# A decoder block's head: parameters packed into the first load, squared tiles summed as they come, root and broadcast ahead of the adaLN rows

## The chip, the core and the metric

The kernel runs on one NeuronCore of a Trainium2 chip. Its engines work side by side, each through its own list of instructions in order: TensorE (PE in the rows: matmuls, with the loads of their stationary operand listed as PEld), VectorE (DVE), ScalarE (ACT), GpSimd (POOL), and SyncE (SP), which here issues nearly all transfers. Sixteen DMA engines move data between HBM and on-chip memory (SBUF); matmuls write to PSUM. An engine waits at an instruction until what the instruction needs is there, and all that stands behind it on that engine waits too. The metric is the device time of one execution in microseconds, lower is better.

## What is computed

One block with an attention-and-convolution mixer and a gated convolutional FFN; 256 positions of 1024 features, all float32. Each half normalises its input and modulates it by a conditioning vector c:

```python
mod = silu(c) @ w_ada[l] + b_ada[l]
sh1, sc1, gt1, sh2, sc2, gt2 = jnp.split(mod[:, None, :], 6, axis=-1)
h = rmsnorm(x, g_mix[l]) * (1.0 + sc1) + sh1          # x / sqrt(mean(x*x) + eps) * g
proj = h @ w_in[l]                                    # q, k, v, u, c_gate, b_gate
...                                                   # attention, short convolution, two norms
x = x + gt1 * (mixed @ w_out[l])
h = rmsnorm(x, g_ffn[l]) * (1.0 + sc2) + sh2
up = causal_dwconv(h @ w_up[l], ffn_conv_w[l], ffn_conv_b[l])
x = x + gt2 * ((silu(gte) * val) @ w_down[l])
return rmsnorm(x, g_final)
```

## The kernel before

Everything lies feature-major: x is `xT`, 128 partitions by 8 tiles of 256 positions. Weights come as 1 MB pieces (q/k/v pieces 768 KB) into a ring of 8 slots; `advance()` issues the next piece on SyncE as soon as the slot it goes to is freed, in the order of the list `order`. At the start that is: adaLN weights of group 0 (`a1`), `wqkv` of tile 0 (q0), `a1` of group 1, q1, two pieces of `a1` for group 2, q2, q3. The first eight pieces are issued at once, q0 and q1 in two transfers each (columns 0 to 1023, then 1024 to 1535). Ahead of them go x in four quarters of two tiles (L91), and, on ScalarE's queue, the first 104 columns of the parameter array `pp` (L90: c, biases, norm weights); its other 176 columns, for the FFN, are loaded at L388.

Large matmuls keep float32 accuracy by splitting each operand into a rounded part (hi) and a rest (lo), and doing three passes: hi*hi, hi*lo, lo*hi (`mm3`). hi is a cast on ScalarE (`split_hi`, `split_hi_q`, or `hhi` for the activations), lo a subtraction on VectorE (`split_lo`, `split_lo_q`, `hlo`). A plain float32 matmul leaves two records in the trace.

The head works as follows. Each engine's order is the order of the statements, since the program is scheduled by hand.
- `keep_clock(n)` runs n matmuls of a constant on TensorE whose result nobody reads; 22 of them at the start.
- ScalarE makes silu(c) (`cs`, L232); VectorE repeats it over 32 columns (`crep`) and adds 1 to two bias columns (`bsc1`). ScalarE squares x a quarter at a time (L242), VectorE adds the quarters up to one tile (L244, L245).
- `ada_rows(g)` (L253): 64 matmul records for shift and scale of one group of tiles; groups are (0), (1), (2, 3), (4, 5), (6, 7). `ada_cols(g)` (L266) turns the rows into columns on VectorE: one transpose and three small operations.
- `add_squares` (L210) sums over the partitions on TensorE; `rms_root` (L216) does the scaling on VectorE and the power -0.5 on GpSimd; `rms_bcast` (L223) spreads the result with two matmuls into PSUM (`psrx`).
- `normed(kt)` multiplies a tile by it on VectorE, `modulated(kt)` makes `hhi` on ScalarE and `hlo` on VectorE.

The order of the statements at L338 to L352 is: rows of group 0, sum of squares, root, columns of group 0, `keep_clock(4)`, three casts and one subtraction for q0, broadcast, `normed(0)`, `modulated(0)`, a copy of the broadcast to SBUF (`rxb`), two more subtractions. Then the loop over the 8 tiles starts (L354): q/k matmuls, with the rows of a later group between them, v matmuls, and the splits of the next tile. `normed(1)` to `normed(7)` read `rxb`.

Of the kernel before, what the change touches and what calls it, by code (L numbers as in the profile page):

```python
# [8 lines left out]
F32 = mybir.dt.float32  # L9
F32R = mybir.dt.float32r  # L10
AF = mybir.ActivationFunctionType
OP = mybir.AluOpType
AX = mybir.AxisListType.X

P = 128
S = 256
D = 1024
A = 512
# [4 lines left out]
KT = D // P  # L23
# [4 lines left out]
PC = {}  # L28
_n = 0
for _name, _w in (("c", 8), ("b_ada", 48), ("g_mix", 8), ("g_ffn", 8), ("g_mixed", 8), ("g_fin", 8),  # L30
                  ("conv_w", 12), ("conv_b", 4), ("ffn_w", 3 * 2 * NJ), ("ffn_b", 2 * NJ)):
    PC[_name] = _n
    _n += _w
NP = _n


FFN_SEQ = [("v", 0), ("g", 0), ("v", 1), ("g", 1), ("v", 2), ("g", 2)]
# [20 lines left out]
def decoder_block(ctx: ExitStack, tc, xT_in, pp, ada1, ada2, wqkv, wst, out):  # L58
# [5 lines left out]
    nc = tc.nc  # L64
    ACT, DVE, PE, POOL = nc.scalar, nc.vector, nc.tensor, nc.gpsimd

    cp = ctx.enter_context(tc.tile_pool(name="cp", bufs=1))
# [15 lines left out]
    def p1(tag, name):  # L83
        return ps1.tile([P, 512], F32, tag=tag, name=name)


    xT = cp.tile([P, KT, S], F32, name="xT")
    par = cp.tile([P, NP], F32, name="par")
    ffn_par = slice(PC["ffn_w"], NP)
    nc.scalar.dma_start(par[:, 0:PC["ffn_w"]], pp[:, 0:PC["ffn_w"]])  # L90
    for i in range(4):  # L91
        nc.sync.dma_start(xT[:, 2 * i:2 * i + 2, :], xT_in[:, 2 * i:2 * i + 2, :])

    def col(name, i):
        o = PC[name] + i
        return par[:, o:o + 1]


    order = []
# [10 lines left out]
    def advance():  # L110
        while state["next"] < len(order):
            i = state["next"]
            if i >= NRAW and order[i - NRAW] not in freed:
                return
            k = order[i]
            t = rawp.tile([P, 2048], F32, tag="raw", name="raw")
            if k[0] == "a1":
                nc.sync.dma_start(t, ada1[GROUPS[k[1]][k[2]]])
            elif k[0] == "q":
                for c in ((slice(0, 2 * A), slice(2 * A, 3 * A)) if k[1] <= 1 else (slice(0, 3 * A),)):  # L120
                    nc.sync.dma_start(t[:, c], wqkv[k[1], :, c])
            elif k[0] == "a2":
                nc.sync.dma_start(t, ada2[k[1], k[2]])
            else:
                nc.sync.dma_start(t, wst[k[1]])
            ring[k] = t
            state["next"] += 1

    def free(k):
        freed.add(k)  # L130
        advance()

    advance()


# [17 lines left out]
    def keep_clock(n, ps=warm):  # L153
        for _ in range(n):
            PE.matmul(ps[:, 0:P], ones, ones, start=True, stop=True)

    keep_clock(22)


    def split_hi(raw, n=1024):  # L160
# [49 lines left out]
    def add_squares(ss, s2, first, last):  # L210

        for t in range(2):
            PE.matmul(ss[:, t * REP:(t + 1) * REP], s2[:, t * P:(t + 1) * P], ones[:, 0:REP], start=(first and t == 0), stop=last,  # L213
                      skip_group_check=True)
# [20 lines left out]
    bsc1 = cp.tile([P, 2, KT], F32, name="bsc1")  # L235
    DVE.tensor_scalar(bsc1[:, 0, :], par[:, PC["b_ada"] + 8:PC["b_ada"] + 16], 1.0, None, op0=OP.add)
    DVE.tensor_scalar(bsc1[:, 1, :], par[:, PC["b_ada"] + 32:PC["b_ada"] + 40], 1.0, None, op0=OP.add)

    pss = p1("v", "pss")
    sqx = cp.tile([P, KT, S], F32, tag="mix", name="sqx")  # L240
    for i in range(4):
        ACT.activation(sqx[:, 2 * i:2 * i + 2, :], xT[:, 2 * i:2 * i + 2, :], AF.Square)  # L242
        if i:
            DVE.tensor_add(sqx[:, 0:2, :], sqx[:, 0:2, :], sqx[:, 2 * i:2 * i + 2, :])  # L244
    DVE.tensor_add(sqx[:, 0, :], sqx[:, 0, :], sqx[:, 1, :])  # L245
    rxb = cp.tile([P, S], F32, tag="sqs0", name="rxb")

    hT = (cp.tile([P, KT, S], F32R, name="hhi"), cp.tile([P, KT, S], F32R, name="hlo"))
    mod1 = cp.tile([P, 2, KT], F32, name="mod1")
# [3 lines left out]
    def ada_rows(g):  # L253


        n = len(GROUPS[g])
        AR[g] = pw(f"psr{g}")[:, 0:64 * n]
        for k in range(KT):
            a = ring["a1", g, k * n // KT].rearrange("p (k j c) -> p k j c", j=4, c=64 * n)
            for j in range(4):  # L260
                PE.matmul(AR[g][32 * j:32 * j + 32, :], crep[:, k, :], a[:, k % (KT // n), j, :],  # L261
                          start=(k == 0), stop=(k == KT - 1))
            if (k + 1) % (KT // n) == 0:
                free(("a1", g, k * n // KT))

    def ada_cols(g):  # L266

        n, kts = len(GROUPS[g]), slice(GROUPS[g][0], GROUPS[g][-1] + 1)
        tr = wk.tile([P, 256], F32, tag="tr", name=f"tr{g}")[:, 0:64 * n]
        DVE.transpose(tr, AR[g])  # L270
        v = tr.rearrange("p (n s q) -> p n s q", s=2, q=32)[:, :, :, 0]
        b = PC["b_ada"] + kts.start
        DVE.tensor_tensor(mod1[:, 0, kts], v[:, :, 1], bsc1[:, 0, kts], op=OP.add)
        DVE.tensor_mul(mod1[:, 0, kts], mod1[:, 0, kts], par[:, PC["g_mix"] + kts.start:PC["g_mix"] + kts.stop])
        DVE.tensor_tensor(mod1[:, 1, kts], v[:, :, 0], par[:, b:b + n], op=OP.add)

    XN = {}
# [11 lines left out]
    def normed(kt, rb):  # L289
        XN[kt] = wk.tile([P, S], F32, tag="xn", name=f"xna{kt}")  # L290
        DVE.tensor_mul(XN[kt], xT[:, kt, :], rb)

    def modulated(kt):
        sc, sh = mod1[:, 0, kt:kt + 1], mod1[:, 1, kt:kt + 1]
        ACT.activation(hT[0][:, kt, :], XN[kt], AF.Identity, bias=sh, scale=sc)
        hf = wk.tile([P, S], F32, tag="cu", name=f"hf{kt}")
        DVE.tensor_scalar(hf, XN[kt], sc, sh, op0=OP.mult, op1=OP.add)
        DVE.tensor_sub(hT[1][:, kt, :], hf, hT[0][:, kt, :].bitcast(F32))
# [6 lines left out]
    def new_q(kt):  # L305
        WQ[kt] = [hip.tile([P, 1024], F32R, tag=t, name=t) for t in ("hi", "lo", "hi", "lo")]
# [20 lines left out]
    def split_hi_q(kt, part):  # L327
        c = slice((part % 2) * 512, (part % 2) * 512 + 512)
        ACT.copy(WQ[kt][part // 2 * 2][:, c], ring["q", kt][:, part * 512:(part + 1) * 512])

    def split_lo_q(kt, part):
        hi, lo = WQ[kt][part // 2 * 2:part // 2 * 2 + 2]
        c = slice((part % 2) * 512, (part % 2) * 512 + 512)
        DVE.tensor_sub(lo[:, c], ring["q", kt][:, part * 512:(part + 1) * 512], hi[:, c].bitcast(F32))
        if part == 2:
            free(("q", kt))

    ada_rows(0)  # L338
    add_squares(pss, sqx[:, 0, :], True, True)
    rx = rms_root(pss, D, "x")  # L340
    ada_cols(0)
    keep_clock(4)
    new_q(0)
    for part in range(3):
        split_hi_q(0, part)
    split_lo_q(0, 0)
    psrx = rms_bcast(rx, pw("psrx"))
    normed(0, psrx)
    modulated(0)
    ACT.copy(rxb, psrx)  # L350
    split_lo_q(0, 1)
    split_lo_q(0, 2)  # L352
    pv += [p1("v", "pv0"), warm]
# [31 lines left out]
                split_q(kt + 1, 1)  # L385
                split_q(kt + 1, 2)

    nc.sync.dma_start(par[:, ffn_par], pp[:, ffn_par])  # L388


    tmpm = wk.tile([P, 384], F32, tag="sp", name="tmpm")
# [219 lines left out]
    for s in range(NS - 2):  # L611

        j, i = divmod(s, 3)
# [251 lines left out]
def _arrange(x, c, w_ada, b_ada, g_mix, w_in, conv_w, conv_b, g_attn_out, g_conv_out,  # L865
             w_out, g_ffn, w_up, ffn_conv_w, ffn_conv_b, w_down, g_final):
    import numpy as np

    def cols(a):
        return np.asarray(a).reshape(-1, P).T  # L870

    def k_major(w):

        return w.reshape(-1, P, w.shape[1]).transpose(1, 0, 2)

    w_ada, b_ada, w_in, w_out, w_up, w_down = (np.asarray(a)[0] for a in (w_ada, b_ada, w_in, w_out, w_up, w_down))
    pp = np.concatenate([cols(a) for a in (c, b_ada, g_mix, g_ffn, g_attn_out, g_conv_out, g_final, conv_w, conv_b,
                                           ffn_conv_w, ffn_conv_b)], axis=1)
    sec = w_ada.reshape(D, 6, D)

    by_k = sec[:, 0:2].reshape(KT, P, 2, KT, 4, 32).transpose(1, 0, 4, 3, 2, 5)
    ada1 = []
    for kts in GROUPS:
        n = len(kts)
        a = by_k[:, :, :, kts[0]:kts[-1] + 1]
        ada1 += [a[:, i * KT // n:(i + 1) * KT // n].reshape(P, 2048) for i in range(n)]
    ada1 = np.stack(ada1)

    ada2 = np.stack([sec[:, s].reshape(4, 2, P, KT, 4, 32).transpose(0, 2, 1, 4, 3, 5) for s in (2, 3, 4, 5)])
    ada2 = ada2.reshape(4, 4, P, 2048)  # L890
    wqkv = w_in[:, :3 * A].reshape(KT, P, 3 * A)

    def piece(w, j):
        if w in "ucb":
            o = (3 + "ucb".index(w)) * A + j * P
            return k_major(w_in[:, o:o + P]).reshape(P, 1024)
        if w in "vg":
            o = "vg".index(w) * DFF + j * P
            return k_major(w_up[:, o:o + P]).reshape(P, 1024)
        return (w_out if w == "o" else w_down)[j * P:(j + 1) * P]  # L900

    wst = np.stack([np.concatenate([piece(*PIECES[2 * i]), piece(*PIECES[2 * i + 1])], axis=1)
                    for i in range(len(PIECES) // 2)])
    xT = k_major(np.asarray(x)[0].T)
    return {"x": xT, "pp": pp, "ada1": ada1, "ada2": ada2, "wqkv": wqkv, "wst": wst}


# [18 lines left out]
```

## Time and profile before

| | us |
|---|---|
| three runs | 339.96, 345.25, 347.67 |
| their median | 345.25 |
| the profiled execution, its own time | 342.16 |
| its span, first to last instruction | 340.3 |

The granted TensorE clock over the span is 0.996. In the profile's rows an instruction has the program line that made it, output and inputs by their tile names (`psr` are adaLN rows, `pss` the sum of x's squares, `psrx` its broadcast, `pq` the q/k accumulators, `warm` the keep-clock target), and its shape as partitions x elements. Matmul records overlap: each lasts longer than its distance to the next, so a run of them is counted by distance. Ends of matmuls are modelled by the profiler.

### The profile page before, as it was taken

To read this page: it belongs to the slowest core of one execution; us is meant where nothing else is said; L and a number is where in the kernel's file an instruction comes from. 1 tells how busy PE (TensorE), PEld (TensorE's weight loads), DVE (VectorE), ACT (ScalarE), POOL (GpSimd) and SP (SyncE) were. 2 spreads that over 40 slices of the span, in tenths; PEclk is the share of its full clock that TensorE was granted. 3 is DMA by queue.
4 is the path that set the end of the run, shared out by engine and by line. 5 is a ranking of instruction groups with operands and counts; after the bars stand their busy time and mean duration, and the time that the engine had idled before them with its cause. 6 is when DMAs were issued, how large, how long until landed. Compare 5 with 4: busy or idle time off the path is not lost.

```text
span 340.3 us, 7158 instructions
## 1 busy us (share of the span) xinstructions
PE 328.0 (96%) x2988; PEld 312.6 (92%) x2988; DVE 249.7 (73%) x433; ACT 190.9 (56%) x334; POOL 18.9 (6%) x31
## 2 busy tenths in 40 slices
PE   8799999999999999899999999999999999999992
PEld 8699999887888999699999999999999999999992
DVE  2566773888885886799878888888677777777754
ACT  4244557777764573568655555555455555555550
POOL 1000000010112303100000000000000000000020
PEclk9999999999999999999999999999999999999998
DMA  7999999788878748535657575767555551000003
GB/s 251 418 417 418 417 421 420 306 302 360 335 297 359 262 160 321 223 117 173 231 194 298 193 305 193 298 204 297 165 207 164 209 169 80 2 2 0 2 0 123
DMA packets 12703, 79.23 MB, mean 233 GB/s; under 512 B 1536, under 2 KB 1920, under 8 KB 4096
## 3 DMA queue, kind: packets, MB, share of 16 engines
q1 hardware_dynamic: 12528, 78.74, 60.9%
q8 instruction: 23, 0.38, 0.4%
q10 hardware_dynamic: 144, 0.05, 0.1%
q14 instruction: 8, 0.07, 0.1%
HBM read 77.74 MB, written 1.05 MB: 231 GB/s over the span
## 4 chain that ended last, share of the span: by engine, by line
PE 93%; DMA 2%; DVE 2%; SPq 0%; ACT 0%; issue 0%; POOL 0%; DVEq 0%
PE pu L201 22%; PE pg L201 18%; PE pod L201 18%; PE pq L201 7%; PE pox L201 7%; PE pc L201 4%; PE pb L201 3%; PE psm L574 2%; PE psr L261 2%; DMA raw<-in_ada 2%; PE warm L201 2%; PE pv L201 2%; PE pss L213 1%; PE pss L455 1%; PE pss L454 1%; PE pso L502 1%
## 5 line engine op out<-in xcount | busy, mean ns | idle before, releaser
L167 DVE TENSOR_TENSOR lo<-raw,hi 128x1024 fp32r<-128x1024 f32 x85 | 103.9, 1228 | 4.8 <-ACT hi L162 4.8
L162 ACT CAST hi<-raw 128x1024 fp32r<-128x1024 f32 x86 | 88.8, 1040 | 0.3 <-PE pox L201 0.3
L201 PE MATMUL pu<-hhi,hi 128*128 128x256 f32 x208 | 58.9, 283 | 1.5 <-ACT hhi L283 1.5
L201 PE MATMUL pu<-hhi,lo 128*128 128x256 f32 x208 | 58.0, 279 | 0.0
L201 PE MATMUL pu<-hlo,hi 128*128 128x256 f32 x208 | 57.8, 279 | 0.0
L201 PE MATMUL pod<-ahi,hi 128*128 128x256 f32 x176 | 49.3, 280 | 0.0
L201 PE MATMUL pg<-hhi,hi 128*128 128x256 f32 x176 | 49.3, 280 | 0.0
L201 PE MATMUL pod<-ahi,lo 128*128 128x256 f32 x176 | 49.1, 279 | 0.0
L201 PE MATMUL pod<-alo,hi 128*128 128x256 f32 x176 | 49.1, 279 | 0.0
L201 PE MATMUL pg<-hhi,lo 128*128 128x256 f32 x176 | 49.1, 279 | 0.0
L201 PE MATMUL pg<-hlo,hi 128*128 128x256 f32 x176 | 49.1, 279 | 0.0
L201 PEld LDWEIGHTS pu<-hhi,hi 128*128 128x128 f32 x208 | 39.0, 188 | 2.9 <-ACT hhi L283 1.7
L201 PEld LDWEIGHTS pu<-hhi,lo 128*128 128x128 f32 x208 | 39.1, 188 | 0.0
L201 PEld LDWEIGHTS pu<-hlo,hi 128*128 128x128 f32 x208 | 38.9, 187 | 0.0
L752 DVE SCALAR_TENSOR_TENSOR fyv<-pu,par,fyv 128x255 f32<-128x255 f32 (+1 forms) x44 | 21.2, 482 | 22.1 <-ACT fyv L746 21.3
L746 ACT ACTIVATE fyv<-pu,par 128x256 f32<-128x256 f32 x22 | 12.4, 565 | 41.9 <-PE pu L201 41.9
L201 PEld LDWEIGHTS pg<-hhi,lo 128*128 128x128 f32 x176 | 33.1, 188 | 0.0
L201 PEld LDWEIGHTS pod<-ahi,lo 128*128 128x128 f32 x176 | 33.1, 188 | 0.0
L201 PEld LDWEIGHTS pg<-hhi,hi 128*128 128x128 f32 x176 | 33.0, 188 | 0.0
L201 PEld LDWEIGHTS pod<-ahi,hi 128*128 128x128 f32 x176 | 33.0, 188 | 0.0
L201 PEld LDWEIGHTS pod<-alo,hi 128*128 128x128 f32 x176 | 32.9, 187 | 0.0
L201 PEld LDWEIGHTS pg<-hlo,hi 128*128 128x128 f32 x176 | 32.9, 187 | 0.0
(151 smaller groups left out, 647.6 us busy)
## 6 DMA issues: line engine op xcount, KB each, us to landing
raw<-in_wst SPq DMA_DIRECT2D x43, 1024.0 KB, 4.9
raw<-in_ada SPq DMA_DIRECT2D x24, 1024.0 KB, 8.2
raw<-in_wqkv SPq DMA_DIRECT2D x6, 768.0 KB, 14.1
xT<-in_x SPq DMA_DIRECT2D x4, 256.0 KB, 4.8
raw<-in_wqkv SPq DMA_DIRECT2D x2, 512.0 KB, 9.4
out<-xT SPq DMA_DIRECT2D x3, 256.0 KB, 2.8
raw<-in_wqkv SPq DMA_DIRECT2D x2, 256.0 KB, 9.6
out<-xT SPq DMA_DIRECT2D x2, 128.0 KB, 2.0
```

The costliest lines, as they stand in the source:

```text
L162: ACT.copy(hi[:, 0:n], raw)
L167: DVE.tensor_sub(lo[:, 0:n], raw, hi[:, 0:n].bitcast(F32))
L201: PE.matmul(o, l[p == 2], r[p == 1], start=start and p == 0, stop=stop and p == 2, skip_group_check=shared)
L213: PE.matmul(ss[:, t * REP:(t + 1) * REP], s2[:, t * P:(t + 1) * P], ones[:, 0:REP], start=(first and t == 0), stop=last, skip_group_check= ...
L261: PE.matmul(AR[g][32 * j:32 * j + 32, :], crep[:, k, :], a[:, k % (KT // n), j, :], start=(k == 0), stop=(k == KT - 1))
L454: PE.matmul(ps[:, 0:128], qT[o:o + DH, p, 0:128], kT[o:o + DH, p, 0:128], start=True, stop=True)
L455: PE.matmul(ps[:, 128:384], qT[o:o + DH, p, 128:256], kT[o:o + DH, p, :], start=True, stop=True)
L502: PE.matmul(ps[o:o + DH, c], vs[:, i, h * DH:(h + 1) * DH], AT["pt", h][:, k], start=(i == 0), stop=(i == 1))
L574: PE.matmul(sacc[s][32 * j:32 * j + 32, 0:256], crep[:, kk, :], a[:, k, j * 256:(j + 1) * 256], start=(kk == 0), stop=(kk == KT - 1))
L746: ACT.activation(Y[w, j], PU[w, j][:, 0:S], AF.Identity, bias=col("ffn_b", f), scale=col("ffn_w", 2 * 2 * NJ + f))
L752: DVE.scalar_tensor_tensor(y[:, d:], ps[:, 0:S - d], col("ffn_w", k * 2 * NJ + f), y[:, d:], op0=OP.mult, op1=OP.add)
```

## The change

x and the first 104 parameter columns become one array in HBM and one tile `xp` in SBUF, the parameters ahead of x in each partition's row; the first of the four loads carries them and x's first quarter, and ScalarE's transfer is gone. The FFN's parameters get a tile of their own, `parf`. q0 is loaded in three transfers of 512 columns. The keep-clock at the start is 8 instead of 22. The squares are made a tile at a time, even tiles on ScalarE and odd ones on VectorE, and each is summed on TensorE at once (with a keep-clock call after each pair but the last); VectorE's additions go. Root, broadcast, the scaling of tile 0 and the copy `rxb` come ahead of group 0's rows, which get a keep-clock of 3 behind them. For one-tile groups two of the three small operations of `ada_cols` become one. q0's second and third cast and all its subtractions come behind tile 0's modulation.

```diff
-    nc.scalar.dma_start(par[:, 0:PC["ffn_w"]], pp[:, 0:PC["ffn_w"]])
+    xp = cp.tile([P, NPX + KT * S], F32, name="xp")
+    par = xp[:, 0:NPX]
+    xT = xp[:, NPX:].rearrange("p (k t) -> p k t", t=S)
+    parf = cp.tile([P, NP - NPX], F32, name="parf")
     for i in range(4):
-        nc.sync.dma_start(xT[:, 2 * i:2 * i + 2, :], xT_in[:, 2 * i:2 * i + 2, :])
+        c = slice(NPX + 2 * i * S if i else 0, NPX + 2 * (i + 1) * S)
+        nc.sync.dma_start(xp[:, c], xT_in[:, c])
...
-                for c in ((slice(0, 2 * A), slice(2 * A, 3 * A)) if k[1] <= 1 else (slice(0, 3 * A),)):
-                    nc.sync.dma_start(t[:, c], wqkv[k[1], :, c])
+                n = (3, 2)[k[1]] if k[1] <= 1 else 1
+                for c in {3: ((0, A), (A, 2 * A), (2 * A, 3 * A)), 2: ((0, 2 * A), (2 * A, 3 * A)), 1: ((0, 3 * A),)}[n]:
+                    nc.sync.dma_start(t[:, c[0]:c[1]], wqkv[k[1], :, c[0]:c[1]])
...
-    keep_clock(22)
+    keep_clock(8)
...
-    for i in range(4):
-        ACT.activation(sqx[:, 2 * i:2 * i + 2, :], xT[:, 2 * i:2 * i + 2, :], AF.Square)
-        if i:
-            DVE.tensor_add(sqx[:, 0:2, :], sqx[:, 0:2, :], sqx[:, 2 * i:2 * i + 2, :])
-    DVE.tensor_add(sqx[:, 0, :], sqx[:, 0, :], sqx[:, 1, :])
+    for d in range(0, KT, 2):
+        ACT.activation(sqx[:, d, :], xT[:, d, :], AF.Square)
+        DVE.tensor_mul(sqx[:, d + 1, :], xT[:, d + 1, :], xT[:, d + 1, :])
+        for e in (d, d + 1):
+            add_squares(pss, sqx[:, e, :], e == 0, e == KT - 1)
+        if d + 2 < KT:
+            keep_clock(1)
...
-        DVE.tensor_tensor(mod1[:, 0, kts], v[:, :, 1], bsc1[:, 0, kts], op=OP.add)
-        DVE.tensor_mul(mod1[:, 0, kts], mod1[:, 0, kts], par[:, PC["g_mix"] + kts.start:PC["g_mix"] + kts.stop])
+        gm = par[:, PC["g_mix"] + kts.start:PC["g_mix"] + kts.stop]
+        if n == 1:
+            DVE.scalar_tensor_tensor(mod1[:, 0, kts], v[:, :, 1], bsc1[:, 0, kts], gm, op0=OP.add, op1=OP.mult)
+        else:
+            DVE.tensor_tensor(mod1[:, 0, kts], v[:, :, 1], bsc1[:, 0, kts], op=OP.add)
+            DVE.tensor_mul(mod1[:, 0, kts], mod1[:, 0, kts], gm)
...
-    ada_rows(0)
-    add_squares(pss, sqx[:, 0, :], True, True)
     rx = rms_root(pss, D, "x")
-    ada_cols(0)
     keep_clock(4)
-    new_q(0)
-    for part in range(3):
-        split_hi_q(0, part)
-    split_lo_q(0, 0)
     psrx = rms_bcast(rx, pw("psrx"))
     normed(0, psrx)
+    ACT.copy(rxb, psrx)
+    ada_rows(0)
+    keep_clock(3)
+    ada_cols(0)
+    new_q(0)
+    split_hi_q(0, 0)
     modulated(0)
-    ACT.copy(rxb, psrx)
+    split_hi_q(0, 1)
+    split_lo_q(0, 0)
+    split_hi_q(0, 2)
     split_lo_q(0, 1)
     split_lo_q(0, 2)
...
-    nc.sync.dma_start(par[:, ffn_par], pp[:, ffn_par])
+    nc.sync.dma_start(parf, pp)
```

## Rows read from the trace of the kernel before

**Rows 1.** Page, span in 40 slices: busy tenths of TensorE and the DMA engines.
```profile
PE   8799999999999999899999999999999999999992
...
DMA  7999999788878748535657575767555551000003
```

**Rows 2.** Chain of waits in order of time, 0 to 60 us: start, us, what.
```profile
0.74 0.38 SPq L92
...
2.58 7.48 DMA raw<-in_ada
...
10.20 1.10 PE psr L261 x64
11.30 0.56 PE pss L213 x4
...
12.96 0.72 PE psrx L226 x4
...
14.16 0.61 ACT hhi L295
...
14.82 1.21 PE pq L201 x8
...
17.06 2.02 PE pq L201 x16
...
21.88 1.88 PE psr L261 x64
...
26.77 2.82 PE pq L201 x24
```

**Rows 3.** DMA issues at 0.74, 7.50 and 10.08: KB each, us from issue to landing.
```profile
xT<-in_x SPq DMA_DIRECT2D x1, 256.0 KB, 4.5
...
raw<-in_ada SPq DMA_DIRECT2D x1, 1024.0 KB, 14.5
...
raw<-in_wqkv SPq DMA_DIRECT2D x1, 768.0 KB, 13.8
```

**Rows 4.** Timelines of ScalarE and VectorE: start, us, what, idle before and releaser.
```profile
5.43 0.21 ACT L232 ACTIVATE cs<-par 128x8 f32<-128x8 f32 x1 [2.98 <-DMA par<-in_pp]
5.54 1.68 ACT L242 ACTIVATE sqx<-xT 128x512 f32<-128x512 f32 x3
7.50 0.63 ACT L242 ACTIVATE sqx<-xT 128x512 f32<-128x512 f32 x1 [0.28 <-DMA xT<-in_x]
...
17.87 0.60 ACT L295 ACTIVATE hhi<-xna,mod 128x256 fp32r<-128x256 f32 x1 [2.85 <-DVE mod L275]
18.38 1.65 ACT L329 CAST hi<-raw 128x512 fp32r<-128x512 f32 x3
...
5.95 0.17 DVE L237 TENSOR_SCALAR bsc<-par 128x8 f32<-128x8 f32 x1
...
17.41 0.16 DVE L273 TENSOR_TENSOR mod<-tr,bsc 128x1 f32<-128x1 f32 x1
17.60 0.16 DVE L274 TENSOR_TENSOR mod<-mod,par 128x1 f32<-128x1 f32 x1
...
25.69 0.43 DVE L298 TENSOR_TENSOR hlo<-hf,hhi 128x256 fp32r<-128x256 f32 x1
```

**Rows 5.** ScalarE's groups by form, 328.5 to 331 us: count, busy us, mean ns, idle.
```profile
L682 ACT ACTIVATE sqr<-xT 128x256 f32<-128x256 f32 x4 | 1.6, 416 | 0.6 <-DVE xT L680 0.6
```

**Rows 6.** TensorE's groups, 1.5 to 6.4 us, then 7 to 9.2 us.
```profile
L155 PE MATMUL warm<-ones 128*128 128x128 f32 x23 | 5.3, 428 | 1.5 <-POOL mhalf L141 1.5
...
L155 PE MATMUL warm<-ones 128*128 128x128 f32 x20 | 2.4, 275 | 0.0
```

**Rows 7.** TensorE's groups by form, 135 to 138.2 us: the second norm's sums.
```profile
L213 PE MATMUL pss<-ones,sqr 128*128 128x16 f32 x16 | 2.0, 264 | 0.0
```

**Rows 8.** Timeline of SyncE: the issues at 7.50 and 10.08.
```profile
7.50 0.33 SPq L118 DMA_DIRECT2D raw<-in_ada  x1
...
10.08 0.33 SPq L121 DMA_DIRECT2D raw<-in_wqkv  x1
```

More of the change, by code (lines that the diff above doesn't have):

```diff
@@ L34 @@
 NP = _n
+NPX = PC["ffn_w"]
 FFN_SEQ = [("v", 0), ("g", 0), ("v", 1), ("g", 1), ("v", 2), ("g", 2)]
@@ L84, in p1 @@
         return ps1.tile([P, 512], F32, tag=tag, name=name)
-    xT = cp.tile([P, KT, S], F32, name="xT")
-    par = cp.tile([P, NP], F32, name="par")
-    ffn_par = slice(PC["ffn_w"], NP)
-    nc.scalar.dma_start(par[:, 0:PC["ffn_w"]], pp[:, 0:PC["ffn_w"]])
+    xp = cp.tile([P, NPX + KT * S], F32, name="xp")
+    par = xp[:, 0:NPX]
+    xT = xp[:, NPX:].rearrange("p (k t) -> p k t", t=S)
+    parf = cp.tile([P, NP - NPX], F32, name="parf")
     for i in range(4):
-        nc.sync.dma_start(xT[:, 2 * i:2 * i + 2, :], xT_in[:, 2 * i:2 * i + 2, :])
+        c = slice(NPX + 2 * i * S if i else 0, NPX + 2 * (i + 1) * S)
+        nc.sync.dma_start(xp[:, c], xT_in[:, c])
     def col(name, i):
         o = PC[name] + i
-        return par[:, o:o + 1]
+        return parf[:, o - NPX:o - NPX + 1] if o >= NPX else par[:, o:o + 1]
     order = []
@@ L903, in _arrange @@
                     for i in range(len(PIECES) // 2)])
-    xT = k_major(np.asarray(x)[0].T)
-    return {"x": xT, "pp": pp, "ada1": ada1, "ada2": ada2, "wqkv": wqkv, "wst": wst}
+    xT = np.concatenate([pp[:, :NPX], k_major(np.asarray(x)[0].T).reshape(P, KT * S)], axis=1)
+    return {"x": xT, "pp": pp[:, NPX:], "ada1": ada1, "ada2": ada2, "wqkv": wqkv, "wst": wst}
 def kernel(**inputs):
```

## The prediction

> **What bounds the kernel now.** I read the page's slices first. TensorE is 90% busy or more in nearly every slice, while the DMA engines are saturated only at the start and half idle later [rows 1]. So a change to the head is worth what it moves the first dense matmul, and the loads can take it back only while they are saturated. The chain of waits, in order of time, says what the head waits for [rows 2]. The first adaLN weights land at 10.06 us; 64 matmuls make the rows (10.20 to 11.30); then x's sum of squares, the power on GpSimd, the broadcast, the scaling on VectorE and the first tile of hhi on ScalarE, and the first q/k matmul starts at 14.82. Behind it the chain is TensorE without a hole. The head is a line: load, rows, squares, root, broadcast, scale. The change takes squares, root and broadcast out of it and puts them in front, into time in which TensorE now runs keep-clock matmuls and then waits for the load.
>
> **The sum, step by step, in the profiled execution's times.**
>
> *First load.* x's first quarter is issued at 0.74 and lands 4.5 us later, at 5.24; for the last ScalarE waits until 7.50. The parameters come by themselves, and the silu waits for them until 5.43 [rows 2 to 4]. Three more quarters in 2.26 us is 0.75 us for 256 KB, so the 52 KB that now ride in front cost 0.15: both land at 5.4. Silu starts where it did. Bounds: 5.24 (the bytes were moving anyway) to 5.6.
>
> *First squares.* Silu takes ScalarE to 5.54 (start of the next instruction there), and a 128x256 square takes 0.42 [rows 4, 5]: tile 0 is ready at 5.96. VectorE still makes crep and two small columns first, to 6.12 [rows 4]; a 128x256 multiply there is 0.43 (an operation of that shape, hlo, is 0.43, [rows 4]), so tile 1 is ready at 6.5. The later tiles wait for their quarters, the last about 7.5 + 0.4 = 7.9.
>
> *Sums on TensorE.* Today one tile is summed, in 4 matmul records; the change sums eight, 32 records, with three keep-clock calls of 2 records between: 38. The 16 output columns do not make a record cheap. Where 16 of them stand without a wait, 15 steps take 2.0 - 0.26 us: 0.116 us each, as much as a keep-clock record of 128 columns (19 steps in 2.4 - 0.28: 0.112) [rows 6, 7]. I take 0.116. Tile 0 from 5.96 to 6.43, a short wait for tile 1, then 34 x 0.116 = 3.94: the last record starts at 10.33 and ends 0.26 later, at **10.6**. That is 2.7 us behind the last square: the adds, not x's loads, set the end. Below: if the sums kept pace with the loads they would end at 8.5.
>
> *Root and broadcast.* From the end of the sum to the broadcast is now 12.96 - 11.86 = 1.10, and the broadcast takes 0.72 [rows 2]: 12.42. The four keep-clock calls behind the sum (8 records, 0.9) fit into the 1.10. The scaling of tile 0 and the copy of the broadcast to SBUF run beside what follows.
>
> *Rows and columns.* ada_rows(0) stands behind the broadcast on TensorE, so it starts at 12.42 though its weights land at 10.06: 1.10 later, 13.52. From rows to hhi I take the second group, where nothing else is late: 17.06 (end of its rows, [rows 2]) to 17.87 is 0.81, less 0.19 for the merged add-and-multiply (17.60 - 17.41) [rows 4]: hhi starts at 14.14. From its start to the first q/k matmul is 0.66 [rows 2]: **14.8 us, against 14.82**. The three keep-clock calls behind the rows (0.7) run inside that wait. The rows have changed places with the squares, and the eightfold sum eats what the root's move frees.
>
> *Moved casts.* The cast of q0's second third now follows hhi on ScalarE; it takes 0.55 (three in 1.65) after the 0.5 that hhi holds it (17.87 to 18.38) [rows 4]. The fifth matmul of the first pass wants it 4 x 0.15 (eight in 1.21, [rows 2]) = 0.6 after the first, which itself starts 0.66 after hhi: it comes at 1.05, wanted at 1.26. Nothing; 0.1 if the matmuls run closer. The three lo's on VectorE move behind hhi too; they are wanted after the second group's rows and a pass, over 2 us on: nothing. If that cover were gone, about 0.6 each, by the casts of the same shape.
>
> *Loads.* Each issue waits for the landing of the one eight before: at 7.50 for x's last quarter, at 10.08 for the first adaLN weights [rows 2, 4, 8]. With the parameters' issue gone and q0 in thirds, the second half of the third adaLN group is issued at 10.1 instead of 7.50. It lands only at 22.0, 14.5 later [rows 3], because the engines are busy with what is ahead; 11.9 us are still enough. Nothing, unless the queue ran dry; then 2.6. The third small issue costs SyncE 0.43 and the transfer a few small packets.
>
> *The rest.* The tile for the FFN's parameters is loaded at the same place; shorter keep-clock at the start saves nothing, TensorE waits then. Sum: 0.0 at the first q/k matmul, 0 to +0.1 after it: **no change, 342.2 us** in the profiled execution. That one is 3 us under the median of the runs, 345.25; on the median the forecast is 345.3.
>
> **The rivals.**
>
> *A. The sum holds* (within 0.5 us).
>
> *B and C. The clock.* The keep-clock records lie 0.22 us apart in the first 4.9 us (5.3 less 0.43 in 22 steps, with a slow first one) and 0.112 after 7: the first is the 1.2 GHz level, the second 2.4 [rows 6]. The page's granted clock does not part the two stretches, so the distance is what to read. TensorE had worked without a pause from 1.51 until the step, which lies past 6.4. The change stops after 16 records, 1.51 + 16 x 0.22 = 5.0, pauses until 5.96 and goes on with narrow sums. So the clock may still be low there. For it: in this trace it was low at 5.0. Against: the sums keep TensorE without a pause as well. Price of a low record: 0.22 - 0.116, about 0.105. Upper end, every record doubles: **B**, the rise comes halfway, 19 x 0.105 = +2.0 (347.3 on the median). **C**, it comes only with the dense work behind the sums: 38 x 0.105 = +4.0 (349.3), and +6 if broadcast and rows are slow too (4 x 0.11, 64 x 0.017, keep-clock 0.6). This one ends on the other side; it decides from about 5 low records on. Lower end: weight loads are as fast at the low level and only the 6 keep-clock records double, +0.7. I take the upper end, as the only low records in the trace have a 128-column load and are doubled.
> The Trainium skill ("TensorE: Matmul & The Clock Gate", Part 1) says the low level is the default and activity lifts it. That is C's mechanism; the step in this trace after unbroken work agrees, and no row here shows what narrow matmuls do. The same page (Part 2, LDWEIGHTS) gives load time as columns over 1.2 GHz with no term for the gate; by that the price would be the lower end, C +0.7 instead of +4.0, and a sum record at the high level 0.107, near the 0.116 of the row.
>
> *D. The sums are cheaper than a record alone* and end with the loads, at 8.5. Then the rows start on their weights at 10.2 and the first q/k matmul at 11.3 + 0.62 + 0.66 = 12.6, 2.2 us earlier. It does not last. The second half of the third group's rows needs the load of 22.0 (now used about 22.8), and the third tile's hlo hangs on q2, landed at 10.08 + 13.8 = 23.9, through cast, lo and hf until 26.12; TensorE gets there now at 26.77 [rows 2, 3, 4]. The saturated loads leave **-0.6**: 344.6. Against it: 0.116 stands in the trace without a wait.
>
> **How the numbers follow.** A 0.52, B 0.18, C 0.20, D 0.10. All four lie within 2% (6.9 us), which is about what a measurement of this kernel can tell from no change: its three runs differ by 7.7 us. I leave 0.03 for faster and 0.05 for slower by over 2%, mostly that spread, and C with the slow rows. The predicted time is A's, 345.3. The range runs from the lowest run, 340.0 (A or D in such runs), to C's 349.3. A alone, against the same execution, is 341.7 to 342.7.
>
> **What would show it.** Right: 32 sum records about 0.116 apart ending near 10.6; broadcast before rows; the first q/k matmul at 14.5 to 15.1; no new wait behind it. B or C: records 0.21 apart after 6 us, and the first q/k matmul at 16 to 20. D: sums ending before 9, then new waits for adaLN weights or q2 at 22 to 26. Wrong altogether: a load that lands over 1 us later than now, or a gap on TensorE after the second tile.

## The result, and the profile after

| | kernel before | changed kernel |
|---|---|---|
| executions timed side by side | 6 | 6 |
| median, us | 342.76 | 345.74 |
| lowest to highest, us | 339.33 to 347.67 | 344.85 to 349.09 |
| profiled execution, us (span) | 342.16 (340.3) | 344.85 (343.1) |

The ratio is 1.0129, with a 95% interval of 1.0082 to 1.0175: within 2%, but slower. Ratios and intervals, here and below, use only a kernel's executions within 1.5% of its fastest, while medians use all of them, so the two can point different ways. The time lies in the predicted range; the sign is that of rivals B and C.

The chain of waits of the changed kernel in order of time (start, us, what), which answers to [rows 2]; its last two lines are the last norm, with the dense work before them left out:

```profile
1.51 3.74 PE warm L159 x16
5.25 0.80 PE pss L217 x8
...
6.37 0.80 PE pss L217 x8
...
8.60 1.51 PE pss L217 x8
10.12 1.89 PE warm L159 x8
12.01 0.85 PE psrx L230 x4
12.86 1.91 PE psr L268 x64
...
15.40 0.61 ACT hhi L306
...
16.06 1.24 PE pq L205 x8
...
28.05 2.83 PE pq L205 x24
...
330.76 2.66 PE pss L217 x20
333.42 2.75 PE warm L159 x12
```

Up to 8.3 us ten records (eight sums, two keep-clock) take 1.12. The last eight sums take 1.51 alone, the eight keep-clock records behind them 1.89, the broadcast 0.85 instead of 0.72 and the rows 1.91 instead of 1.10. The stretches of TensorE say why (stretch, its length, busy time and records, granted clock, DMA share, GB/s):

```profile
5.20:8.40 3.20, 3.20 (x31) 1.00 1.00 369
8.60:15.20 6.60, 6.60 (x86) 0.50 1.04 421
15.40:20.00 4.60, 4.44 (x91) 1.00 1.00 410
```

The clock went up near 5.1, as the first sums began, and down again near 8.5, while TensorE was never idle. From there to 15.3 the last sums, keep-clock, broadcast and rows run at the 1.2 GHz level.

| landmark, us | before | after | difference |
|---|---|---|---|
| first q/k matmul | 14.82 | 16.06 | +1.24 |
| third tile's matmuls | 26.77 | 28.05 | +1.28 |
| last norm's sums | 329.51 | 330.76 | +1.25 |
| span | 340.3 | 343.1 | +2.8 |

So 1.25 us come from the head and pass through 300 us of dense work unchanged. The other 1.55 arise in the last norm, where the instructions are the same in both kernels. There the clock fell too, at the end of the 20 narrow sums, and in the execution of before it did not (330 to 336, first the changed kernel):

```profile
329.30:332.70 3.40, 3.06 (x28) 1.00 0.00 0
332.80:336.10 3.30, 3.30 (x17) 0.50 0.00 0
```
```profile
332.80:336.10 3.30, 1.00 (x9) 1.00 0.23 78
```

Executions of either kernel differ in where the clock steps, so their times are compared below by medians, and heads by landmarks. (In the profiled execution of `e10_after_again` the granted clock stood at 0.75 from 18 us to the end, span 412 us; only its first 18 us are read.) Over all jobs the kernel before has a median of 343.27 (110 executions, 338.82 to 349.15), the changed kernel 345.05 (11, without that one): 1.8 us slower.

### The profile page after: what moved, and what is told of

Same layout as the page of the kernel before. It is cut to its first block, busy times and chain, and to the rows that moved or that the text cites. A ratio compares the mean times of both kernels' runs of the same rounds, so it can differ in the third digit from the quotient of the medians.

```text
span 343.1 us, 7177 instructions
## 1 busy us (share of the span) xinstructions
PE 333.1 (97%) x3000; PEld 317.7 (93%) x3000; DVE 248.4 (72%) x431; ACT 190.3 (55%) x334; POOL 18.9 (6%) x31
## 4 chain that ended last, share of the span: by engine, by line
PE 96%; DVE 1%; ACT 0%; POOL 0%; issue 0%; DVEq 0%; POOLq 0%
PE pu L205 22%; PE pg L205 18%; PE pod L205 18%; PE pq L205 7%; PE pox L205 7%; PE pc L205 4%; PE pb L205 3%; PE warm L159 3%; PE psr L268 3%; PE pss L217 2%; PE psm L586 2%; PE warm L205 2%; PE pv L205 2%; PE pss L467 1%; PE pss L466 1%; PE pso L514 1%
## 5 line engine op out<-in xcount | busy, mean ns | idle before, releaser
L764 DVE SCALAR_TENSOR_TENSOR fyv<-pu,parf,fyv 128x255 f32<-128x255 f32 (+1 forms) x44 | 21.2, 482 | 22.1 <-ACT fyv L758 21.3
L758 ACT ACTIVATE fyv<-pu,parf 128x256 f32<-128x256 f32 x22 | 12.4, 564 | 41.9 <-PE pu L205 41.9
```

The costliest lines, as they stand in the source:

```text
L758: ACT.activation(Y[w, j], PU[w, j][:, 0:S], AF.Identity, bias=col("ffn_b", f), scale=col("ffn_w", 2 * 2 * NJ + f))
L764: DVE.scalar_tensor_tensor(y[:, d:], ps[:, 0:S - d], col("ffn_w", k * 2 * NJ + f), y[:, d:], op0=OP.mult, op1=OP.add)
```

## Experiments

There were two theories at first. **Clock**: narrow sums let the clock fall, and what stands behind them pays. **Order**: rows behind an eightfold sum and a broadcast are simply a longer line. One question stood beside them: x's first quarter landed at 3.52, not at the 5.4 of the forecast.

### Wide sums of x's squares, e1 and e12

```diff
-    def add_squares(ss, s2, first, last):
+    def add_squares(ss, s2, first, last, rep=REP):
...
-            PE.matmul(ss[:, t * REP:(t + 1) * REP], s2[:, t * P:(t + 1) * P], ones[:, 0:REP], ...
+            PE.matmul(ss[:, t * rep:(t + 1) * rep], s2[:, t * P:(t + 1) * P], ones[:, 0:rep], ...
...
-            add_squares(pss, sqx[:, e, :], e == 0, e == KT - 1)
+            add_squares(pss, sqx[:, e, :], e == 0, e == KT - 1, P)
```

> The changed kernel with one edit: the sums of x's squares have 128 output columns instead of 16 (same values in all of them, the root reads one). Clock theory (narrow sums let the clock fall at 8.49 us, and the keep-clock, the broadcast and the rows behind them run at the 1.2 GHz level): a sum record costs 0.116 us as before, the clock stays up once it has risen, the sums end near 9.4 instead of 10.1, the broadcast starts 1.1 later (10.5 instead of 12.01), rows take 1.1 instead of 1.9, and the first q/k matmul starts near 13.6 instead of 16.06; of these 2.5 us the loads leave about 2 (the third group's second piece lands at 21.7), so the time is some 2 us (0.6%) below the changed kernel's. Order theory (what costs is that rows now stand behind an eightfold sum and the broadcast, at any clock): the first q/k matmul within 0.5 us of 16.06, time unchanged or higher.

> The changed kernel with wide sums of x's squares, once more. If narrow sums were what cost: median 2 to 5 us below the 345.3 to 345.7 of the changed kernel, at or up to 2 us below the kernel before; if the first result was luck with the two matmul distances: median at 344 or above.

Medians 340.39 (12 executions) and 343.44 (12), ratios to the kernel before 0.9939 (0.9893 to 0.9986) and 0.9919 (0.9869 to 0.997). Together the median is 341.81, 3.2 us below the changed kernel's. The first lies further below it than the 2 us expected; the second is at the upper end of what was expected, and 0.15 above the kernel before in its own job (343.29). Such medians depend on the two matmul distances told of below. The heads are clear. In e12's the clock rose at 5.2 and stayed through the head (chain, then stretches):

```profile
5.29 0.93 PE pss L217 x8
...
6.44 0.89 PE pss L217 x8
...
8.68 0.91 PE pss L217 x8
...
10.68 0.71 PE psrx L230 x4
11.39 1.07 PE psr L268 x64
...
13.75 1.25 PE pq L205 x8
...
25.97 2.98 PE pq L205 x24
```
```profile
5.30:15.00 9.70, 9.02 (x132) 1.00 1.03 407
15.00:30.00 15.00, 15.00 (x210) 1.00 1.01 415
```

The sums end at 9.6, rows take 1.07, the first q/k matmul comes at 13.75 instead of 16.06. In e1's profiled execution the clock rose later, at 7.6, and it came at 14.88. The same records at the same distance, 128 columns wide instead of 16, kept the clock in both. The other experiments agree. In all four profiles with wide sums of x (e1, e4, e8, e12) the granted clock was 1.00 from its rise, between 4.9 and 7.6, to 140 us at least. Of the four in which eight tiles were summed with 16 columns, three lost it during the sums (the changed kernel, e3, e7) and one had not gained it by 17.9 (e10). In e12, of 2.3 us gained at the first q/k matmul, 2.1 are left at the third tile.

### More keep-clock ahead, narrow sums kept, e7

```diff
-    keep_clock(8)
+    keep_clock(22)
```

> The changed kernel with 22 instead of 8 keep-clock calls at the start, narrow sums kept. Rival to the narrow sums: the clock is lost because the first dense stretch is too short. If so: the clock, once up, stays up; the sums start near 8 to 9 and end near 13, first q/k matmul near 16.5, but none of the slow executions; median near or below the changed kernel's 345.7. Narrow-sum theory: the clock rises within the keep-clock and falls during the sums all the same, which now end near 13 to 15; first q/k matmul at 17 to 19, median 1 to 3 us above 345.7.

Median 347.46 (6), ratio 1.0171 (1.0099 to 1.0243). The clock rose within the keep-clock and fell during the sums (chain, then stretches):

```profile
8.30 0.80 PE pss L217 x8
...
11.65 1.32 PE pss L217 x8
12.97 1.89 PE warm L159 x8
14.87 0.85 PE psrx L230 x4
15.72 1.87 PE psr L268 x64
...
18.94 1.23 PE pq L205 x8
```
```profile
5.00:11.60 6.60, 6.60 (x62) 1.00 1.03 401
11.80:18.50 6.70, 6.70 (x86) 0.50 1.03 419
```

So the short dense stretch at the start is not what costs. The first q/k matmul at 18.94 is where the narrow-sum theory had it.

### The changed kernel again, e10

Nothing is edited.

> The changed kernel unchanged, for a second profile and more executions. Its six runs had three mean clocks: 0.98 (343.1 to 343.2 us span), 0.996 (344.6), 0.987 (347.3). The clock theory reads them as where in the head the clock steps: up early and down at 8.5 (first q/k matmul 16.0); never up before the dense work behind the sums (first q/k matmul 17 to 19); up early, down later than 8.5 or down again elsewhere. A second profile should show one of these, with sum records 0.2 us apart wherever the clock is low, and the median should stay 2 to 4 us above that of the kernel before. If the first profile was a chance: records at 0.1 us, first q/k matmul near 14.

Median 345.31 (6; 344.85 without the profiled execution, which took 413.94), ratio 1.01 (1.0019 to 1.0182). In that profile the clock never rose ahead of the dense work:

```profile
5.29 1.52 PE pss L217 x8
6.81 0.61 PE warm L159 x2
7.42 1.52 PE pss L217 x8
...
13.21 1.89 PE warm L159 x8
15.10 0.85 PE psrx L230 x4
15.96 1.91 PE psr L268 x64
...
19.15 1.36 PE pq L205 x8
```

Ten records take 2.13 us from first to last group, 0.213 each, twice the 0.112 of the first profile. That is what rival C describes: 38 records low, broadcast and rows low behind them, first q/k matmul at 19.15, 4.3 us behind the kernel before. But this is the execution whose clock stood at 0.75 from 18 us on; whether an ordinary execution of the changed kernel has such a head is not shown.

### The packed load alone, e2 and e11; parameters first on the same queue, e9

e2 and e11 are the kernel before with `xp` and `parf` as in the change and nothing else. In e9 the parameters keep their own transfer of 416-byte rows, ahead of x on SyncE's queue:

```diff
-    nc.scalar.dma_start(par[:, 0:PC["ffn_w"]], pp[:, 0:PC["ffn_w"]])
+    nc.sync.dma_start(par[:, 0:PC["ffn_w"]], pp[:, 0:PC["ffn_w"]])
```

> The kernel before with the packed first load alone. In the changed kernel x's first quarter landed at 3.52 us instead of 5.25, and the first adaLN weights at 9.26 instead of 10.06. If the packing does this (a second queue with 416-byte rows held up the first loads): landings at about 3.5 and 9.3, rows start at 9.4, first q/k matmul near 14.1 instead of 14.82, time 0.3 to 0.7 us below the kernel before. If it is something else in the change (or chance of that execution): landings at 5.2 and 10.0, first q/k matmul at 14.8, no difference.

> The kernel before with the parameters' load issued on SyncE's queue ahead of x instead of on ScalarE's, otherwise as it was (416-byte rows, a transfer of its own). Packed, x's first quarter landed at 3.5 us instead of 5.25 and the first adaLN weights at 9.5 instead of 10.06. If it was the second queue beside x that held the first loads up: parameters land near 3.2, x's first quarter near 4.0, first adaLN weights near 9.6 to 9.8 (one more issue of 0.4 us in front), first q/k matmul near 14.4. If it was the small rows: parameters and x's first quarter at 5 or later, adaLN weights at 10.1 or later, first q/k matmul at 14.9.

> The kernel before with the packed first load, once more: in all profiles so far the time between 240 us and 320 us is one of two (113.3 or 117.8 ns from one matmul to the next, some 3 us), whatever the kernel, so 12 executions are too few for a median. If the packing is worth 0.6 us (its third tile starts at 26.20 instead of 26.77) median 0.3 to 2.5 us below the kernel before of the same job; the fastest execution near 338.1 against 338.8.

Timelines of ScalarE, first e2, then e9, against 5.43 and 5.54 in [rows 4]:

```profile
3.51 0.21 ACT L234 ACTIVATE cs<-xp 128x8 f32<-128x8 f32 x1 [1.50 <-DMA xp<-in_x]
3.62 0.61 ACT L244 ACTIVATE sqx<-xp 128x512 f32<-128x512 f32 x1
```
```profile
2.58 0.21 ACT L232 ACTIVATE cs<-par 128x8 f32<-128x8 f32 x1 [0.56 <-DMA par<-in_pp]
5.22 1.37 ACT L242 ACTIVATE sqx<-xT 128x512 f32<-128x512 f32 x2 [2.43 <-DMA xT<-in_x]
```

The second queue is not it: with the parameters first on x's own queue they land at 2.6, yet x's quarter still comes only at 5.2, and the first q/k matmul at 15.19; the median is that of the kernel before (343.48 against 343.19, ratio 1.0027, 0.9963 to 1.0092). Nor do the small rows explain it as was expected: by that reading the parameters too had to come at 5 or later. What stands is that x's first quarter lands 2.7 to 2.9 us after its issue in every profile with the packed load, and 4.5, 3.7 and 4.0 after it in those without (before, e5, e9). The Trainium skill ("DMA: Bandwidth & Descriptors", Specifications) puts the least size for full rate at 512 bytes, with a read-modify-write below it. Rows of 416 bytes are on that side and the direction agrees, but the parameters' own packets are too little: in the kernel before they take 3.5% of the 16 engines' first 10 us, 0.35 us. In e9, with the parameters landed, the engines move 74 and 94 GB/s in the two halves of the microsecond from 3.0 to 4.0, against 404 and 320 in e2. What holds x's quarter up stays open. The packing also sets x's rows in HBM 8608 bytes apart instead of 8192, and no run parts that from the transfer it removes.

The chain of e2 carries the gain on:

```profile
2.57 6.92 DMA raw<-in_ada
...
14.24 1.21 PE pq L203 x8
...
26.20 2.82 PE pq L203 x24
```

0.58 us at the first q/k matmul, 0.57 at the third tile. Medians 340.44 and 341.93 against 342.62 and 343.29 in the same jobs, ratios 0.9954 (0.9913 to 0.9995) and 0.9954 (0.9905 to 1.0002). That is 1.4 to 2.2 us, more than the 0.57 of the landmarks; what the rest is stays open. In e11's profile the clock fell in this head too (0.50 from 11.7 to 18.4, first q/k matmul 15.07, third tile 28.53). So a head in the order of the kernel before can lose the clock too. There TensorE had waited 1.56 us for the weights and then run rows and four narrow sums; which of these did it was not tested.

### Rows ahead of the broadcast, e3, and with wide sums, e4

```diff
-    keep_clock(4)
-    psrx = rms_bcast(rx, pw("psrx"))
-    normed(0, psrx)
-    ACT.copy(rxb, psrx)
     ada_rows(0)
-    keep_clock(3)
     ada_cols(0)
+    psrx = rms_bcast(rx, pw("psrx"))
+    normed(0, psrx)
+    ACT.copy(rxb, psrx)
```

> The changed kernel with group 0's rows and columns ahead of the broadcast again (behind the sums), without the two keep-clock calls there. Order theory: rows (1.1 to 1.9 us) run while the power is made, the scaling hangs on the broadcast alone, first q/k matmul 2 us earlier than 16.06, near 14.0, time about 1.5 to 2 us below the changed kernel's. Clock theory: the clock still falls after the narrow sums, so the rows still take 1.9 us and the broadcast 0.85; the rows only take the place of the keep-clock, so the first q/k matmul also comes near 14.0, but with rows at the 0.03 us distance; the order then is a price of its own beside the clock. If neither matters: 16.06.

> Both edits: sums with 128 columns, and rows ahead of the broadcast. If clock and order both cost: sums end near 9.4, rows 9.5 to 10.6, broadcast 10.6 to 11.3, first q/k matmul near 12.4 to 12.8. From there the loads decide (third group's second piece at 21.7, q2 at 23.6): at most 1 us below the kernel before, 2.5 to 3.5 us below the changed kernel. If only one of them costs, no better than the better of the two single edits.

e3: median 344.64 (12), ratio 1.0051 (1.0004 to 1.0099), 0.4 to 1.1 us under the changed kernel. The granted clock was 0.50 from 7.8 to 18; rows took 1.87, and the first q/k matmul came at 15.05, not 14.0: `rxb` and a cast of q0 stand between the scaling and hhi on ScalarE (0.9 us), which the expectation forgot. Of the 1.0 us gained on the changed kernel nothing is left at the third tile (28.31 against 28.05), since the clock stayed low to 18.0 instead of 15.3.

e4 has both: rows 9.41, broadcast 10.49, first q/k matmul 13.14 (12.4 to 12.8 was expected). Against e12's 13.75, with the clock up in both, order is worth 0.6 us: a price, a small one beside the clock. Median 340.73 (12), ratio 0.996 (0.9919 to 1.0001), no better than e1. The waits of TensorE between 12 and 26 us, and its chain, show where the head's gain goes:

```profile
PE psr L268 <- DMA raw<-in_ada: 0.9, 1, 0.9
```
```profile
9.38 12.77 DMA raw<-in_ada
...
22.19 1.08 PE psr L268 x32
...
26.28 1.78 PE pq L205 x15
```

TensorE waits 0.86 us for the second half of the third group's weights. From 1.7 us at the first q/k matmul 0.5 are left at the third tile. e2 (26.20), e4 (26.28) and e12 (25.97) reach it together, with first q/k matmuls at 14.24, 13.14 and 13.75.

### Wide sums everywhere, e5, e6, e8

```diff
-REP = 16
+REP = P
```

in the kernel before (e5), in it with the packed load (e6), and in the changed kernel (e8).

> The kernel before with 128 columns instead of 16 in all its sums of squares (x's, the two mixer norms, the FFN norm, the final norm); nothing else. Clock theory carried to the kernel before: its runs spread from 338.9 to 348.7 us because narrow sums late in the kernel (16 records near 136 us, 20 near 330) let the clock fall in some executions; wide sums cost the same 0.116 us each and keep it up: the median falls by 1 to 2.5 us from 342.6 and the slowest runs stay below 346. Against it (the spread has another cause): median and spread as before.

> The kernel before with the packed first load and with 128 columns in all sums: a candidate to beat both kernels. The packed load alone gave a median of 340.44 us. If clock and load add up: 338 to 339.5, spread under 5 us. If the spread does not come from the sums: 340.4 again.

> The changed kernel with 128 columns in all sums, where the first experiment had them for x alone (340.39 us). If the falls late in the kernel come from narrow sums too: 338 to 339.5 and a spread under 5 us, as the packed load with wide sums in the kernel before; the order of the change is then worth less than 1 us either way, since the loads at 21 to 24 us take back what the head gains.

Medians 343.9, 341.78 and 341.96 against 344.55 for the kernel before in that job; ratios 1.0033 (0.9995 to 1.0071), 1.0002 (0.9946 to 1.0058), 0.9993 (0.9951 to 1.0035). All three expectations of the median were too good. The upper half was right: no execution above 344.5, 343.7 and 343.4, where the kernel before went to 347.6. The clocks agree: over the whole execution the granted clock was 0.991 to 0.998 in each of these 36, and below 0.991 in 20 of the 29 executions of the kernel before in that job.

The last norm shows one place. From its first sum to the end of its broadcast it takes 4.30 us where the clock holds (before, e2, e11) and 5.0 to 5.9 where it falls. Leaving out e10, it falls in seven of the ten profiles with narrow sums there: the changed kernel, e1, e3, e4, e7, e12, and e9, which has the head of the kernel before:

```profile
327.02 2.41 PE pss L213 x20
329.43 2.05 PE warm L155 x12
331.48 0.87 PE psrb L226 x4
```

With wide sums it falls in none of the three (e5, e6, e8), and the norm takes 4.37.

What sets the lower end of the times is something else. Between about 238 and 320 us the same matmuls run at one of two distances. A part of the chain of before, then the same part of e12:

```profile
258.52 2.83 PE pg L201 x24
261.35 2.83 PE pod L201 x24
```
```profile
258.76 2.72 PE pg L205 x24
261.48 2.72 PE pod L205 x24
```

2.83 us for 24 (117.8 ns each) or 2.72 (113.3). Over some 28 such groups that is 3 us, which fits the gap between about 339 and 342 that most kernels' executions show. Profiles of e3, e6, e9, e11 and e12 have the short one, those of before, after, e1, e2, e4, e5, e7 and e8 the long one, at a granted clock of 1.00 in both. What chooses was not found; it does not go by the change.

The ratios of e1, e2 and e12 have intervals that end below 1; none is 2% faster. Over 24 executions each, the packed load alone has a median of 340.62 and the change with wide sums of x 341.81, against 342.98 for the kernel before in the same two jobs. For the second the two jobs differ (2.2 us below, 0.15 above), so that it beats the kernel before is not shown.

## Why the forecast was half right

**What bounds the kernel**: right. A shift of the first q/k matmul is found again 300 us later.

**First load**: wrong by 1.9 us. The step priced the 52 KB that were added to x's first quarter and took the removed transfer for nothing. Packed, the quarter lands at 3.5; what had held it up in the kernel before is open.

**First squares, start of the sums**: 5.1 instead of 5.96, since the data was there; the low keep-clock, ending at 5.2, was the last to come.

**Price of a sum record**: right at the high level (1.12 for ten), and so was "the adds set the end": in e12 x is complete by 6.6 and the sums end at 9.6.

**The clock**: this is the step that failed. The sum took every record at the high level, with a chance of 0.52. In the first profile 8 sums and all that follows to 15.3 were low, in the second all 38. The forecast's "against" (the sums keep TensorE without a pause) was no reason: TensorE was busy 6.60 of 6.60 us while low. Of the two bounds for a low record the upper was right, as the only low rows had it: 0.213 against 0.112 with 16 columns, and in e1, where the first eight sums of 128 columns were low, 0.214. C's low broadcast and rows were priced too high: in the changed kernel they cost 0.13 and 0.81 us more, not 0.44 and 1.1. The Trainium skill ("TensorE: Matmul & The Clock Gate", Part 2, LDWEIGHTS) has no term for the gate in the load time; here the load records of the sums last 192 ns at the high level (e12) and 333 at the low one (e10), and the measurement decides. Part 1's rule that the low level is the default and activity lifts it agrees with the rise near 5.1. What the runs add is the fall: behind sums of 16 columns the clock fell with TensorE busy throughout, and with sums of 128, the only difference in e1 and e12, it did not.

**Root and broadcast**: right with the clock held (9.58 to 10.68 in e12, 1.10). At the low level the four keep-clock calls took 1.89, did not fit into those 1.10 and held the broadcast up by some 0.8.

**Rows, columns, hhi**: right. From the end of the sums to the first q/k matmul the forecast has 4.20; with the clock held it is 4.15 in e12 (9.6 to 13.75). Its "rows have changed places with the squares" is the small price of order that e4 shows.

**Moved casts, moved issues**: right, nothing. The piece that is issued later (9.27 instead of 7.50) lands at 21.7 instead of 22.0.

**D's cap**: right, on the path of e4: a head 1.7 us earlier, a wait for the third group's second piece, 0.5 left.

**The total**: two errors cancelled in part. Where the clock held (e12) the first q/k matmul came at 13.75, 1.07 us earlier than in the kernel before, since x and with it the sums came early; the forecast had no change. The lost clock added 2.3 to that in the changed kernel. What came is B to C, which had 0.38 together, against 0.52 for no change. That the measured median, 345.74, lies 0.4 from the forecast 345.3 is luck: the forecast added nothing to 345.25, a median of three executions, and the kernel before has 342.76 over the six timed beside the change and 343.27 over all 110.

The other 1.55 of the 2.8 us between the two profiled executions come from the last norm. The change is not needed for them, as e9 loses the clock there with the head of the kernel before; but of the ten profiles with narrow sums there the six built on the changed kernel all lost it, and of the four built on the kernel before one did, so whether the change makes it likelier stays open.

## What to carry to other kernels

With a 128-column load, a matmul with 16 output columns stood as far from the next here as one with 128 (ten records in 1.12 us either way, 5.25 to 6.37 and 6.44 to 7.56), and eight tiles summed by the narrow ones left the clock low for what stood behind. Where the load sets the distance, widening the output cost nothing here, so try it. Try packing a small first transfer into the large one beside it, too: here the large one then landed 0.8 to 1.8 us sooner after its issue. And look up what lands next before making a head shorter: what it gains beyond that load is waited away.

## What the runs showed of the hardware that was not expected

- The granted clock fell to 0.50 with TensorE busy in every microsecond (8.60 to 15.20, 6.60 of 6.60 us).
- x's first quarter, 256 KB, landed 2.7 to 2.9 us after its issue with 52 KB of parameters packed into its rows, and 3.7 to 4.5 after it with the parameters in a transfer of their own, of 128 rows of 416 bytes, on another queue or ahead on the same one.
- With sums of 128 columns everywhere the mean granted clock of 36 executions was 0.991 or more; with 16 columns (the kernel before, same job) it was below that in 20 of 29.
- The same float32r matmuls ran 117.8 or 113.3 ns apart through some 80 us, at the same granted clock.
